# Seven half-size products for the down-projection of the two middle chunks of each FFN, with H and Y kept in memory meanwhile

## The chip, the cores and the metric

The kernel runs on one core of one Trainium2 chip. The metric is the device time of an execution in microseconds (us), as the median of several runs. A NeuronCore has the matrix engine TensorE (PE; its weight loads are listed apart as PEld), the vector engine DVE, the scalar engine ACT, GpSimd (POOL) and the sync engine SP. SBUF is the on-chip memory of 128 partitions, PSUM its accumulator of eight banks, and sixteen DMA engines move data between SBUF and device memory. SP issues the plain transfers here, POOL those that add to what lies at their destination.

## The reference

A decoder trunk of two layers over 528 tokens (16 meta tokens and 512 tokens) with model width 1024 in float32. Each layer has two half-step SwiGLU FFNs of width 2816 around a mixer (gated linear attention in layer 0, sliding-window attention in layer 1). The change touches the FFNs, of which there are four:

```python
def rmsnorm(x, g):
    xf = x.astype(jnp.float32)
    y = xf * lax.rsqrt(jnp.mean(xf * xf, axis=-1, keepdims=True) + EPS)
    return (y * g.astype(jnp.float32)).astype(x.dtype)

def swiglu(x, w_in, w_out):
    gate, up = jnp.split(x @ w_in, 2, axis=-1)
    return (jax.nn.silu(gate) * up) @ w_out
...
    for layer in range(DEPTH):
        g = norm_gains[layer]
        h = h + 0.5 * rmsnorm(swiglu(rmsnorm(h, g[0]), w_ffn_in[layer, 0], w_ffn_out[layer, 0]), g[1])
        hn = rmsnorm(h, g[2])
...
        h = h + rmsnorm(mix, g[3])
        h = h + 0.5 * rmsnorm(swiglu(rmsnorm(h, g[4]), w_ffn_in[layer, 1], w_ffn_out[layer, 1]), g[5])
```

## The kernel before

**Layout.** Everything is kept transposed: 128 rows of the model width on the partitions, tokens along the free axis. `H` (the residual stream) and `Y` (the output of a sub-layer before its norm) are fixed SBUF tiles of eight row blocks x 528 tokens each. All other large operands are tiles of two rows x 528 columns from one pool, `pair_tile` (L162), with `SLOTS` = 32 slots. Matrix products are made in three parts: each operand is split into a rounded high part and the remainder, by an ACT copy and a DVE subtraction, and TensorE runs high x high, low x high and high x low (`mm3s`, L350; one line, L177, issues nearly all matmuls).

**Weights.** All weights are listed in `units` in the order of use. `prefetch` (L316) and `load_unit` (L287) issue their transfers ahead of use into 13 raw tiles of 512 columns; `split_unit` and `split_pair` (L251) split them into pool tiles. `set_ahead` sets how far ahead, and for a pair how many split parts may be alive (`RING` = 10). At most two pairs (`CHAINS`) are in preparation at a time.

**An FFN** (`ffn`, L764) cuts its 22 tiles of the inner width into four chunks (4, 6, 6 and 6 tiles). The first chunk computes gate and up by plain products of two token groups (272 and 256 columns in layer 0, two of 256 or one of 512 in layer 1), while `right_factors` (L832) prepares the fourteen tiles `z` from `H`. The other three chunks use Strassen's scheme in Winograd's form (`class Strassen`, L877): a tile of gate and the tile of up beside it are the two rows of a 2 x 2 block product over the two halves of the model width and the two halves of the tokens, so that seven products of half size (four steps of k, three matmuls each, 264 or 256 columns) take the place of eight. A weight pair is loaded as five raw tiles, two of them summed by accumulating transfers from POOL (L299), and further sums are made on DVE (`add`, L265). `head`, `body` and `tail` issue the seven products of a tile; the head of the next tile is issued between body and tail. The products go onto the banks `a`, `c` (two of each, taken in turns) and `d`; ACT copies them out at L910, L916, L918 and L920, and the job `gated` forms silu(gate) x up and splits it into the tile `hid`.

**Down-projection.** After each chunk `out_steps` (L668) multiplies the chunk's 4 or 6 `hid` tiles with the weights of `w_out` for eight row blocks, over all tokens. The first chunk's result is copied to `Y` (L705), later ones are added to it by DVE (L707). For a chunk of six tiles these are 8 x 6 x 3 = 144 matmuls over each token group. In the last chunk the norm of the output and the residual follow (`Residual.run`, L513), which read `Y` and `H`. In GLA `Y` also holds the values `v`, and in the attention of layer 1 the first four score tiles lie in it.

**Order.** TensorE's order is the program's. The order of program pieces that belong to different tiles comes from `Flow` (L62), a list of jobs with an estimated clock. A job can be delayed by a number it yields, and `flow.wait` runs other jobs until one is done. The other engines run their instructions in the order that the scheduler of the framework made at compile time.

Of the kernel before, what the change touches and what calls it, by code (L numbers as in the profile page):

```python
# [9 lines left out]
F32 = mybir.dt.float32  # L10
# [6 lines left out]
P = 128  # L17
# [14 lines left out]
SLOTS = 32  # L32
# [3 lines left out]
CHAINS = 2  # L36

# [102 lines left out]
def trunk_kernel(ctx: ExitStack, tc, a, out, last_out):  # L140
# [10 lines left out]
    H = cp.tile([P, KD, TOK], F32, name="H")  # L151
    Y = cp.tile([P, KD, TOK], F32, name="Y")
# [16 lines left out]
    def flat(t):  # L169
        return t.rearrange("p a t -> p (a t)")  # L170

# [22 lines left out]
    for layer in range(2):  # L194
        for f in range(2):
            for lo, hi in FF_CHUNKS:
# [3 lines left out]
                if lo < LAST:  # L200
                    units += [a["w_out"][layer, f, m, :, lo * P : hi * P] for m in range(KD)]
                else:
                    units += [a["w_last"][layer, f, i] for i in range(NLAST)]
# [47 lines left out]
    def split_pair(i, raws):  # L251


        r11, r12, r22, s1, s3 = raws
        parts, ready = loaded[i]

        def part(name, src):
            yield from slot(i)
            w = pair_tile(f"w{i}_{name}")
            act.activation(w[:, 0, :512], src, AF.Copy)  # L260
            dve.tensor_tensor(w[:, 1, :512], src, w[:, 0, :512].bitcast(F32), op=ALU.subtract)  # L261
# [10 lines left out]
        add(r11, s1)  # L272
        yield STEP
        yield from part("s2", r11)
        yield STEP
        yield from part("12", r12)
        add(r12, r11)
        yield STEP
        yield from part("s3", s3)
# [7 lines left out]
    def load_unit():  # L287
# [3 lines left out]
        if isinstance(units[i], list):  # L291
            g, u = units[i]
            chains[0] += 1
            a11, a12, a21, a22 = (b[:, c : c + 512] for b in (g, u) for c in (0, 512))
            r11, r12, r22, s1, s3 = raws = [raw_tile(f"raw{i}_{k}") for k in range(5)]
            for r, src in ((s1, a21), (s3, a21), (r11, a11), (r12, a12), (r22, a22)):
                sp.dma_start(r, src)
            for r, src in ((s1, a22), (s3, a11)):
                pool.dma_start(r, src, accum_op=ALU.add)  # L299
            dma_end[0] = max(dma_end[0], flow.clock) + 7 * 512 * 1.5e-3  # L300
            names = ("11", "12", "22", "s1", "s2", "s3", "s4")
            loaded.append(({k: [] for k in names}, {k: Job(None) for k in names}))
            gen = split_pair(i, raws)
# [364 lines left out]
    def out_steps(hid, groups, split_groups, first, finish=None, tailm=0, packed=False, jobs=(), second=(), late=1):  # L668
# [71 lines left out]
        for m in range(KD - tailm):  # L740
# [4 lines left out]
            for gi in range(len(accs)):  # L745
                sq(m, gi)
# [882 lines left out]
```

## Time and profile before

| what | value |
|---|---|
| median of 3 runs | 1875.4 us (1875.31 to 1875.67) |
| the profiled execution's own time | 1875.26 us |
| its span | 1873.5 us |
| instructions | 37758 |
| moved by DMA | 231.37 MB, mean 123 GB/s |
| DMA queues by kind | q1 plain (SP), q0 from POOL, others small |

The page gives busy time, share of the span and number of instructions for each engine, then 40 slices, the DMA queues, the chain of work that ended last (followed back from the end, with the share of the span by engine and by line) and the costliest groups of instructions. A group's row has the line, the engine, the operation, output <- input, the tile form, the count, busy time in us and the mean duration of one in ns, and then the idle time of the engine just before those instructions with what released it. A matmul's duration in ns is its whole way through the array, so the mean is longer than the distance from one matmul to the next. In the chain listed in order of time each row has its start, its length, the engine, the tile written, the line and the number of instructions. In the list of DMA issues the last number is the median time from issue to landing.

### The profile page before, as it was taken

How to read it: one execution, taken by the hardware profiler on the slowest of the kernel's cores; microseconds unless marked ns; L12 is line 12 of the kernel's file. 1: busy time of each engine (PE TensorE's matmuls, PEld its weight loads, DVE VectorE, ACT ScalarE, POOL GpSimd, SP SyncE). 2: the span in 40 equal slices, each digit the busy share in tenths (PEclk: the TensorE clock that was granted, in tenths of full speed). 3: DMA queues.
4: the chain of work that ended last, by engine and by line, in shares of the span. 5: the costliest groups of instructions: out<-in, count | busy, mean ns of one | idle time of the engine just before them, and what ended most of it. 6: DMA issues, size and time to landing. Idle time of an engine off the chain costs nothing.

```text
span 1873.5 us, 37758 instructions
## 1 busy us (share of the span) xinstructions
PE 1864.1 (99%) x14463; PEld 1785.1 (95%) x14463; DVE 1306.0 (70%) x2693; ACT 1022.4 (55%) x2309; POOL 289.2 (15%) x439
## 2 busy tenths in 40 slices
PE   9999999999999999999999999999999999999998
PEld 9999999999999999999999898989988898989898
DVE  7874747767564787474787875757777679758584
ACT  5662636654446566262674563636667866636264
POOL 2101010330001410101033101010220141010102
PEclk9999999999999999999999999999999999999999
DMA  6556565421113255556552456565421224565651
GB/s 209 150 136 150 148 152 151 134 69 57 60 66 113 57 136 140 142 150 150 155 178 57 102 133 172 134 171 146 147 75 52 68 56 120 146 153 157 149 151 46
DMA packets 133381, 231.37 MB, mean 123 GB/s; under 512 B 15312, under 2 KB 27472, under 8 KB 133200
## 3 DMA queue, kind: packets, MB, share of 16 engines
q1 hardware_dynamic: 112032, 190.62, 31.6%
q0 software_dynamic: 20736, 37.76, 12.8%
q8 instruction: 113, 1.85, 0.4%
q14 instruction: 68, 0.56, 0.1%
q10 hardware_dynamic: 432, 0.59, 0.1%
HBM read 226.28 MB, written 2.10 MB: 122 GB/s over the span
## 4 chain that ended last, share of the span: by engine, by line
PE 94%; DVE 3%; ACT 1%; issue 1%; POOL 1%; DMA 0%; SPq 0%; DVEq 0%; POOLq 0%
PE y L177 31%; PE a L177 22%; PE x L177 17%; PE c L177 10%; PE d L177 6%; PE o L177 1%; PE e L177 1%; PE po L177 1%; PE sa L177 1%; PE pt L189 1%; DVE w L242 1%; PE ps L177 0%; ACT w L241 0%; PE sb L177 0%; DVE gu L781 0%
## 5 line engine op out<-in xcount | busy, mean ns | idle before, releaser
L299 POOL DMA_DIRECT2D raw<-in_w_in x144 | 125.8, 908 | 962.7 <-DMA raw<-in_w_in 609.0
L177 PE MATMUL y<-hidl0f,w 128*128 128x256 f32 (+1 forms) x2112 | 262.4, 285 | 1.1 <-DVE hidl0f L454 0.9
L177 PEld LDWEIGHTS y<-hidl0f,w 128*128 128x128 f32 x2112 | 259.3, 188 | 2.2 <-DVE hidl0f L454 1.5
L242 DVE TENSOR_TENSOR w<-raw,w 128x512 fp32r<-128x512 f32 x376 | 234.3, 653 | 35.4 <-ACT w L241 33.0
L261 DVE TENSOR_TENSOR w_s<-raw,w_s 128x512 fp32r<-128x512 f32 x288 | 197.9, 688 | 77.3 <-ACT w_s L260 75.4
L177 PE MATMUL y<-hidl1f,w 128*128 128x512 f32 (+1 forms) x1344 | 250.6, 346 | 0.5 <-DVE hidl1f L454 0.4
L177 PEld LDWEIGHTS y<-hidl1f,w 128*128 128x128 f32 x1344 | 212.2, 188 | 35.0 <-ACT hidl1f L942 0.9
L241 ACT ACTIVATE w<-raw 128x512 fp32r<-128x512 f32 x376 | 206.7, 587 | 52.6 <-PE y L177 34.3
L260 ACT ACTIVATE w_s<-raw 128x512 fp32r<-128x512 f32 x288 | 179.6, 625 | 82.1 <-PE y L177 44.5
L261 DVE TENSOR_TENSOR w<-raw,w 128x512 fp32r<-128x512 f32 x216 | 145.5, 688 | 57.6 <-ACT w L260 53.5
L260 ACT ACTIVATE w<-raw 128x512 fp32r<-128x512 f32 x216 | 130.8, 623 | 44.1 <-PE y L177 42.8
L177 PE MATMUL x<-x_l0m,w 128*128 128x272 f32 (+1 forms) x1152 | 152.1, 288 | 0.0
L707 DVE TENSOR_TENSOR Y<-y,Y 128x256 f32<-128x256 f32 (+2 forms) x175 | 82.0, 475 | 96.4 <-PE y L177 95.4
L177 PEld LDWEIGHTS x<-x_l0m,w 128*128 128x128 f32 x1152 | 143.3, 188 | 2.7 <-issue 1.7
L448 POOL TENSOR_TENSOR acc_post<-acc_post,sq_post 128x256 f32<-128x256 f32 (+1 forms) x77 | 62.8, 816 | 456.0 <-ACT sq_post L447 455.3
L177 PE MATMUL a<-zl0f_t,w_s 128*128 128x264 f32 x864 | 117.4, 285 | 0.0
L177 PE MATMUL a<-zl1f_t,w_s 128*128 128x256 f32 x864 | 113.8, 281 | 0.0
L177 PEld LDWEIGHTS a<-zl0f_t,w_s 128*128 128x128 f32 x864 | 110.3, 188 | 0.0
L177 PEld LDWEIGHTS a<-zl1f_t,w_s 128*128 128x128 f32 x864 | 107.4, 188 | 0.3
L266 DVE TENSOR_TENSOR raw<-raw,raw 128x512 f32<-128x512 f32 x144 | 98.9, 687 | 0.5
L177 PE MATMUL x<-x_l0f,w 128*128 128x256 f32 (+1 forms) x768 | 97.5, 287 | 0.5 <-DVE w L242 0.5
L177 PEld LDWEIGHTS x<-x_l0f,w 128*128 128x128 f32 x768 | 94.8, 188 | 1.3 <-DVE w L242 0.9
(514 smaller groups left out, 3316.9 us busy)
## 6 DMA issues: line engine op xcount, KB each, us to landing
raw<-in_w_in SPq DMA_DIRECT2D x424, 256.0 KB, 3.6
raw<-in_w_in POOLq DMA_DIRECT2D x144, 256.0 KB, 4.9
raw<-in_w_out SPq DMA_DIRECT2D x96, 256.0 KB, 3.3
raw<-in_w_last SPq DMA_DIRECT2D x48, 256.0 KB, 2.9
raw<-in_gla_in SPq DMA_DIRECT2D x48, 256.0 KB, 3.3
raw<-in_w_out SPq DMA_DIRECT2D x64, 128.0 KB, 2.5
raw<-in_gla_out SPq DMA_DIRECT2D x16, 256.0 KB, 2.8
raw<-in_w_q SPq DMA_DIRECT2D x16, 256.0 KB, 4.1
```

The lines of the kernel that those rows point to most:

```text
L177: inst = pe.matmul(o, lhs, rhs, start=start, stop=stop, skip_group_check=onto)
L189: pe.transpose(o, src, ident)
L241: act.activation(w[:, 0, :m], raw[:, :m], AF.Copy)
L242: dve.tensor_tensor(w[:, 1, :m], raw[:, :m], w[:, 0, :m].bitcast(F32), op=ALU.subtract)
L260: act.activation(w[:, 0, :512], src, AF.Copy)
L261: dve.tensor_tensor(w[:, 1, :512], src, w[:, 0, :512].bitcast(F32), op=ALU.subtract)
L266: dve.tensor_tensor(dst, dst, src, op=ALU.add)
L299: pool.dma_start(r, src, accum_op=ALU.add)
L448: pool.tensor_tensor(sums[0][:, :n], sums[0][:, :n], t[:, :n], op=ALU.add)
L707: dve.tensor_tensor(y, p[:, :n], y, op=ALU.add)
```

## The change

- **Seven half-size products for the down-projection.** For the chunks of tiles 4 to 9 and 10 to 15 of each FFN, `hid` is no longer a list of six tiles with their splits. Two neighbouring tiles form a `Step`: the two row halves of a 2 x 2 block, whose columns are the two halves of the tokens. `Step.first` and `Step.second` form the seven right-hand factors from it (four pool tiles f per Step, of six slots with the scratch tiles hk and ht). An item `Down` then computes two row blocks of the output (four items for the eight) by seven products with three steps of k each. Its weight pairs `w_down` are loaded as four raw tiles of 384 columns without accumulating transfers; the sums are made by DVE (`summed` false).
- **Place.** The chunk's four `Down` items come in one list `plan` with the gate-up tiles: after the first tile of the next chunk (`BEFORE_DOWN` = 1). Head, body and tail interleave as before. The first chunk and the last keep the old down-projection.
- **Adding in memory.** `Down` evacuates its banks by ACT into two tiles `t1` and `t2`; POOL issues transfers that add them into `y_sum` and `y_right`, two tensors in device memory (`y_right` is only the right half of the tokens, and the first write of each FFN sets it). `Y` of the first chunk is written to `y_sum` beforehand (`keep`).
- **H and Y.** They are no longer fixed tiles but `Rows`: four pool tiles each, of a pool that now has 40 slots. `H` is written to `h_kept` from `right_factors`, and `H` and `Y` are read back after the tail of the fourth item from the end of the plan (`len(plan) - 4`; three gate-up tiles remain), with `y_right` added to `Y` by POOL. `V` in GLA and the first four score tiles of the attention take pool tiles in place of `Y`.

`class Strassen` keeps its banks and becomes the frame for `Gated` (the former head, body and tail) and `Down`, which share `Item` with `product` and `head`.

```diff
-SLOTS = 32
+SLOTS = 40
...
+BEFORE_DOWN = 1
...
+    dp = ctx.enter_context(tc.tile_pool(name="dp", bufs=1, space=bass.MemoryType.DRAM))
...
+    class Rows:
+        def __init__(self, name):
+            self.name, self.age = name, 0
+            self.fresh()
+
+        def fresh(self):
+            self.age += 1
+            self.tiles = [None] * (KD // 2)
+
+        def pair(self, q):
+            if self.tiles[q] is None:
+                self.tiles[q] = pair_tile(f"{self.name}{self.age}_{q}", F32)
+            return self.tiles[q]
+
+        def __getitem__(self, index):
+            rows, k, cols = (*index, slice(None))[:3]
+            if isinstance(k, slice):
+                assert k.start % 2 == 0 and k.stop == k.start + 2
+                return self.pair(k.start // 2)[rows, :, cols]
+            return self.pair(k // 2)[rows, k % 2, cols]
+
+    H, Y = Rows("H"), Rows("Y")
+    h_kept, y_sum, y_right = (dp.tile([P, KD, TOK], F32, name=f"kept_{nm}") for nm in ("h", "y", "yr"))
...
+                    if ci > 1 and t == lo + BEFORE_DOWN - 1:
+                        units += [[a["w_down"][layer, f, ci - 2, m], a["w_down"][layer, f, ci - 2, m + 1]] for m in range(0, KD, 2)]
+                if lo == 0:
+                    units += [a["w_out"][layer, f, m] for m in range(KD)]
+            units += [a["w_last"][layer, f, i] for i in range(NLAST)]
...
+            r11, r12, s1, r22 = raws
+            s3 = r11
...
+            add(s3, s1)
+            add(s1, r22)
+            s2 = s3
...
+            m = g.shape[-1] // 2
+            summed = m == 512
...
+                raws = [raw_tile(f"raw{i}_{k}")[:, :m] for k in range(4)]
+                for k in (2, 0, 1, 3):
+                    sp.dma_start(raws[k], (a11, a12, a21, a22)[k])
...
+            if keep and m % 2:
+                tok = slice(groups[0][0], groups[-1][0] + groups[-1][1])
+                pool.dma_start(y_sum[:, m - 1 : m + 1, tok], Y[:, m - 1 : m + 1, tok])
...
+        out_proj(hids, groups, x.groups, True, jobs=jobs, keep=True)
+        flow.wait(factors)
+        set_ahead(16, RING)
+        tiles = Strassen(z, halves)
+        plan = []
+        steps = [[Step(tiles, f"{x.name}_{c}{i}") for i in range((hi - lo) // 2)] for c, (lo, hi) in enumerate(FF_CHUNKS[1:3])]
+        for c, (lo, hi) in enumerate(FF_CHUNKS[1:]):
+            for t in range(hi - lo):
+                plan.append(lambda c=c, t=t: Gated(tiles, steps[c][t // 2] if c < 2 else None, t % 2))
+                if c and t == BEFORE_DOWN - 1:
+                    plan += [lambda c=c, q=q: Down(tiles, steps[c - 1], q, c == 1) for q in range(KD // 2)]
+        lo, hi = FF_CHUNKS[-1]
+        hids, jobs = [], []
+
+        def begin(item):
+            t = item()
+            if isinstance(t, Gated) and t.step is None:
+                t.into(new_hid(lo, hids))
+            t.head()
+            return t
+
+        cur = begin(plan[0])
+        for i in range(len(plan)):
+            last = i == len(plan) - 1
+            if last:
+                proj = out_steps(hids, groups, x.groups, False, finish, KD, True, jobs)
+                end = used[0] + NLAST + tail
+            cur.body((lambda: next(proj)) if last else (lambda: None))
+            nxt = None if last else begin(plan[i + 1])
+            job = cur.tail(last)
+            if job is not None:
+                jobs.append(job)
+            cur = nxt
+            if i == len(plan) - 4:
+                H.fresh()
+                Y.fresh()
+                for q in range(KD // 2):
+                    rows, tok = slice(2 * q, 2 * q + 2), slice(o, o + 2 * n2)
+                    sp.dma_start(Y[:, rows, tok], y_sum[:, rows, tok])
+                    sp.dma_start(H[:, rows, tok], h_kept[:, rows, tok])
+                    pool.dma_start(Y[:, rows, right], y_right[:, rows, right], accum_op=ALU.add)
+        set_ahead(32)
...
+        for q in range(KD // 2):
+            rows, tok = slice(2 * q, 2 * q + 2), slice(o, o + 2 * n)
+            sp.dma_start(h_kept[:, rows, tok], H[:, rows, tok])
...
+    class Step:
+        def __init__(self, tiles, name):
+            self.n, self.name, self.parts = tiles.n, name, {}
+            self.done, self.h = Job(None), None
+
+        def rows(self, i):
+            n = self.n
+            if i == 0:
+                self.h, self.t = (pair_tile(f"{nm}{self.name}", F32) for nm in ("hk", "ht"))
+            g, v = (slice(c, c + n) for c in ((n, 0) if i else (0, n)))
+            return self.h[:, i, g], self.h[:, i, v], flat(self.t)[:, (2 + i) * n : (3 + i) * n]
+
+        def split(self, names, src, sign):
+            w = pair_tile(f"f{self.name}_{names[0]}")
+            m = src.shape[-1]
+            act.activation(w[:, 0, :m], src, AF.Copy, scale=sign)
+            if sign == 1.0:
+                dve.tensor_tensor(w[:, 1, :m], src, w[:, 0, :m].bitcast(F32), op=ALU.subtract)
+            else:
+                dve.scalar_tensor_tensor(w[:, 1, :m], src, sign, w[:, 0, :m].bitcast(F32), op0=ALU.mult, op1=ALU.subtract)
+            for i, nm in enumerate(names):
+                self.parts[nm] = [w[:, a, i * self.n : (i + 1) * self.n] for a in range(2)]
+
+        def first(self):
+            self.split(["11"], self.h[:, 0, : self.n], -1.0)
+
+        def second(self):
+            n, h, t = self.n, self.h, flat(self.t)
+            dve.tensor_tensor(
+                t[:, : 2 * n].rearrange("p (a c) -> p a c", c=n),
+                h[:, 0, n : 2 * n].unsqueeze(1).to_broadcast([P, 2, n]), h[:, :, :n], op=ALU.subtract,
+            )
+            yield 0.5
+            self.split(["t1", "t3"], t[:, : 2 * n], 1.0)
+            yield 0.7
+            dve.tensor_tensor(t[:, 2 * n : 3 * n], h[:, 1, :n], t[:, :n], op=ALU.subtract)
+            dve.tensor_tensor(t[:, 3 * n : 4 * n], h[:, 1, n : 2 * n], t[:, 2 * n : 3 * n], op=ALU.subtract)
+            yield 0.7
+            self.split(["t2", "t4"], t[:, 2 * n : 4 * n], 1.0)
+            yield 0.7
+            self.split(["22", "21"], h[:, 1, : 2 * n], -1.0)
+            self.done.finish(flow)
...
+            for k in range(self.nk):
                 wh, wl = (w[:, i, k * P : (k + 1) * P] for i in range(2))
-                xh, xl = (self.z[right][k // 2][:, i, k % 2] for i in range(2))
+                xh, xl = self.right(right, k)
                 mm(bank, wh, xh, first and k == 0, False, not first)
                 mm(bank, wl, xh, False, False, not first)
-                mm(bank, wh, xl, False, k == 3, not first)
+                mm(bank, wh, xl, False, k == self.nk - 1, not first)
...
+                if self.step is not None:
+                    if self.i:
+                        yield from self.step.second()
+                    else:
+                        self.step.first()
+                    return
...
+    class Down(Item):
+        nk = 3
+
+        def __init__(self, tiles, steps, q, new):
+            super().__init__(tiles)
+            self.steps, self.q, self.new = steps, q, new
+            self.t1 = pair_tile(f"dn{self.name}", F32)
+            if q % 2 == 0:
+                tiles.t2 = pair_tile(f"dr{self.name}", F32)
+            self.t2 = tiles.t2[:, q % 2]
+
+        def right(self, name, k):
+            flow.wait(self.steps[k].done)
+            return self.steps[k].parts[name]
+
+        def body(self, between):
+            n = self.n
+            self.product(self.c, "s1", "t1", True)
+            act.activation(self.t2[:, n : 2 * n], self.c, AF.Copy, scale=-1.0)
+            self.product(self.a, "s2", "t2", False)
+            act.activation(self.t2[:, :n], self.a, AF.Copy)
+            self.product(self.d, "12", "21", False)
+            act.activation(self.t1[:, 0, :n], self.d, AF.Copy)
+            self.product(self.a, "s3", "t3", False)
+            act.activation(self.t1[:, 1, n : 2 * n], self.a, AF.Copy, scale=-1.0)
+
+        def tail(self, last):
+            n, o = self.n, self.tiles.o
+            rows, tok, right = slice(2 * self.q, 2 * self.q + 2), slice(o, o + 2 * n), slice(o + n, o + 2 * n)
+            self.product(self.c, "s4", "22", False)
+            act.activation(self.t1[:, 0, n : 2 * n], self.c, AF.Copy)
+            self.product(self.a, "22", "t4", False)
+            act.activation(self.t1[:, 1, :n], self.a, AF.Copy, scale=-1.0)
+            released[0] += 1
+            t2 = self.t2[:, : 2 * n].rearrange("p (a c) -> p a c", c=n)
+            if self.new:
+                pool.dma_start(y_right[:, rows, right], t2)
+            else:
+                pool.dma_start(y_right[:, rows, right], t2, accum_op=ALU.add)
+            pool.dma_start(y_sum[:, rows, tok], self.t1[:, :, : 2 * n], accum_op=ALU.add)
...
+            V = Rows("V")
...
+                    scores[i] = flat(pair_tile(f"s{u}_{hf}", F32))[:, :580]
...
+    c["w_out"] = wo[:, :, :, :, : FF_CHUNKS[0][1]].reshape(2, 2, KD, P, FF_CHUNKS[0][1] * P)
+    c["w_down"] = np.stack([
+        np.concatenate([wo[:, :, :, :, lo + i : hi : 2] for i in range(2)], axis=4) for lo, hi in FF_CHUNKS[1:3]
+    ], axis=2).reshape(2, 2, 2, KD, P, 6 * P)
```

More of the change, by code (lines that the diff above doesn't have):

```diff
@@ L195, in trunk_kernel @@
         for f in range(2):
-            for lo, hi in FF_CHUNKS:
+            for ci, (lo, hi) in enumerate(FF_CHUNKS):
                 for t in range(lo, hi):
@@ L832, in right_factors @@
+        set_ahead(32)
+        cap[0] = min(end, len(units))
+        for _ in proj:
+            pass
     def right_factors(x, halves, z, plain):
@@ L889, in product, with __init__ @@
+    class Item:
+        def __init__(self, tiles):
+            self.tiles, self.n, self.d = tiles, tiles.n, tiles.d
+            i = tiles.count % 2
+            tiles.count += 1
+            self.a, self.c = tiles.a[i], tiles.c[i]
+            self.pair, self.name = next_pair(), used[0]
+        def product(self, bank, left, right, first):
+            parts, ready = self.pair
             flow.wait(ready[left])
             w = parts[left][0]
-            for k in range(4):
+            for k in range(self.nk):
```

201 lines of the change are left out of this document (98 added, 103 removed).

## The prediction

> **What bounds the kernel now.** I read the page's first part, then the chain that ended last, then the stretches.
>
> ```profile
> PE 1864.1 (99%) x14463; PEld 1785.1 (95%) x14463; DVE 1306.0 (70%) x2693; ACT 1022.4 (55%) x2309; POOL 289.2 (15%) x439
> PE 94%; DVE 3%; ACT 1%; issue 1%; POOL 1%; DMA 0%; SPq 0%; DVEq 0%; POOLq 0%
> ```
>
> TensorE is busy for 1864.1 of 1873.5 us and is 94% of the chain: what it does not have to multiply is saved, as long as operands still arrive. The 9.4 us in which it is idle are all that better overlap could win. The chain in order of time (start, length, what) gives its pace, for the first layer's third chunk and for the same chunk of the second layer:
>
> ```profile
> 185.37 2.92 PE a L177 x24
> 226.27 2.91 PE a L177 x24
> 242.80 33.21 PE y L177 x273
> 282.01 2.92 PE a L177 x24
> ...
> 1175.56 2.83 PE a L177 x24
> 1215.24 2.83 PE a L177 x24
> 1236.42 26.85 PE y L177 x114
> 1269.09 2.83 PE a L177 x24
> ```
>
> From 185.37 to 226.27 lie four tiles of a gate-up product by sevenths: 10.225 us each, and with 7 x 12 = 84 matmuls a tile, 121.7 ns per matmul of 264 columns. In the second layer it is 39.68 / 4 = 9.92 us, 118.1 ns for 256 columns. A chunk is 282.01 - 185.37 = 96.64 us, of which six tiles take 61.35; its down-projection takes 35.29 (288 matmuls). In the second layer 93.53 - 59.52 = 34.01 us (144 matmuls of 512 columns).
>
> **The half-size products.** One chunk of a down-projection is now four row pairs x 7 products x 9 matmuls = 252 of 264 (256) columns. At the chain's pace that is 30.67 us, or 29.76 in the second layer: 4.62 and 4.25 us less. Each layer has four such chunks: 4 x (4.62 + 4.25) = **35.5 us**. The groups by form would say otherwise:
>
> ```profile
> L177 PE MATMUL y<-hidl1f,w 128*128 128x512 f32 x768 | 180.5, 394 | 0.5 <-DVE hidl1f L454 0.4
> L177 PE MATMUL a<-zl1f_t,w_s 128*128 128x256 f32 x864 | 113.8, 281 | 0.0
> ```
>
> 180.5 / 768 = 0.235 us for 512 columns, 113.8 / 864 = 0.132 for 256, so that two halves would be dearer than a whole and the second layer would win only 144 x 0.235 - 252 x 0.132 = 0.6 us a chunk, 4 x (4.62 + 0.6) = 20.9 us in all. But such a busy time counts the tail of each product together with the start of the next bank's; the spacing in the chain has no such overlap, and I take it. Nine matmuls in place of twelve change nothing: each has its own weight load either way.
>
> The span lies 1.76 us under that execution's 1875.26, which itself is 0.14 under the median of 1875.4. With everything hidden: 1875.26 - 35.5 = 1839.8.
>
> **What DVE and ACT get to do.** Windows by stage (length, then busy time of PE, PEld, DVE, ACT, POOL, clock, DMA share):
>
> ```profile
> 185.40:236.50 51.10, 51.10 (x422) 51.10 (x421) 40.56 (x73) 32.42 (x71) 3.46 (x4) 1.00 0.52 145
> 236.50:282.00 45.50, 45.50 (x376) 45.50 (x375) 21.81 (x45) 12.18 (x25) 7.01 (x8) 1.00 0.64 152
> ```
>
> ```profile
> 207.71 0.43 DVE L923 TENSOR_TENSOR c<-a,c 128x264 f32<-128x264 f32 x1
> 208.05 0.68 DVE L261 TENSOR_TENSOR w<-raw,w 128x512 fp32r<-128x512 f32 x1
> 208.65 0.69 DVE L261 TENSOR_TENSOR w_s<-raw,w_s 128x512 fp32r<-128x512 f32 x1
> ```
>
> Back to back, a DVE operation on 264 columns holds the engine 0.34 us and one on 512 columns 0.60; I put 0.47 for 384 and 0.62 for 528. A Down item has 7 weight splits and 4 additions of 384 columns: 5.2 us of its 63 x 121.7 ns = 7.67 us. A Step (two gate-up tiles) has 0.34 + 4 x 0.62 + 2 x 0.34 = 3.5 us in place of two splits of 0.62: +2.3. Removed in a chunk are 8 split pairs of 512 and 256 (7.5 us) and 16 additions into Y (5.4). DVE goes from 62.4 of 96.6 us to 62.4 - 12.9 + 4 x 5.2 + 3 x 2.3 = 77.2 of 92.0 us, 84%. ACT:
>
> ```profile
> L241 ACT ACTIVATE w<-raw 128x512 fp32r<-128x512 f32 x312 | 182.6, 622 | 18.9 <-PE y L177 14.9 <-PE e L177 2.0 <-DVE hidl1f L943 1.5
> L241 ACT ACTIVATE w<-raw 128x256 fp32r<-128x256 f32 x64 | 26.4, 412 | 33.7 <-PE y L177 19.4 <-PE a L177 11.8 <-ACT c L933 1.1
> L918 ACT ACTIVATE c<-a 128x264 f32<-128x264 f32 x36 | 13.7, 380 | 0.1
> ```
>
> A split of 384 is some 0.50 us (between 0.41 and 0.585), an evacuation 0.38: 6.2 us for a Down item. With about 1 us more a Step, ACT has 44.6 - 8.0 + 24.8 + 3 = 64 of 92 us. Neither becomes the bound on average, and TensorE's matmuls cover both. Locally three places are tight:
> - The first Down item comes one gate-up tile after the last Step's second tile. Its second product needs t1 after 4 + 2 products of twelve and one of nine, 9.9 us; the Step's own work after that tile is 3.8 us of DVE, and the rest of DVE's work there 79% of 9.9. Together that is 1.7 us too much, unless weight splits made ahead (ten slots) give way. Between 0 and 1.7 us, I take 0.5; eight starts: 4 us.
> - `a` is emptied by ACT while TensorE does the one product "12", and then "s3" goes onto it. The evacuation ends 0.42 us before that today:
>
> ```profile
> 204.81 0.37 ACT L918 ACTIVATE c<-a 128x264 f32<-128x264 f32 x1
> 205.60 1.63 PE L177 MATMUL a<-zl0f_t,w_s 128*128 128x264 f32 x12
> ```
>
>  With nine matmuls "s3" comes 0.37 us sooner and ACT's split before it is 0.1 shorter: 0.15 us is left. Between 0 and 0.2 us lost per item; 0.1 x 32 = 3 us.
> - Tiles: 14 of z, 12 f, ten weight parts, hk, ht and f11 of the next Step, two t1 and one or two t2 make 42 or 43 for 40 slots. The ring then runs two or three short; a product frees one every 1.10 us. It is in the 0.5 above.
>
> **What the DMA engines get to do.**
>
> ```profile
> q1 hardware_dynamic: 112032, 190.62, 31.6%
> q0 software_dynamic: 20736, 37.76, 12.8%
> ```
>
> Share x 1873.5 / MB: a plain MB takes 3.11 us of all 16 engines, an accumulating one 6.35. A gate-up pair (1.311 plain, 0.524 accumulated) is 7.40 us. Old chunk: 6 x 7.40 + 8 x 0.393 x 3.11 = 54.2 of 96.6 us; the windows' 0.52 and 0.64 give 55.7, so this holds. New: 44.4 + 4 x 0.786 x 3.11 + 4 x (0.541 + 0.270) x 6.35 = 74.8 of 92.0 us. Accumulating in memory is nowhere in this trace. Its nearest rows are a write to memory and an accumulation in SBUF:
>
> ```profile
> out<-H SPq DMA_DIRECT2D x4, 256.0 KB, 2.8
> raw<-in_w_in POOLq DMA_DIRECT2D x144, 256.0 KB, 4.9
> ```
>
> Below: the price of a plain transfer, 64.3 us. Above: a read, a write and an accumulation one after the other, about twice 6.35, 95.4 us, which is more than the chunk. I take 6.35 (nearest: same queue, same operation) and no cost. On POOL's queue each of these transfers waits for ACT's last evacuation, and raw additions for the next pairs stand behind it; those are issued well ahead, as the next rows show.
>
> **H and Y back.** SP's issues before the last chunk's end:
>
> ```profile
> 282.08 24.32 SPq L297 DMA_DIRECT2D raw<-in_w_in  x12
> 306.67 20.79 SPq L310 DMA_DIRECT2D raw<-in_w_last  x12
> ```
>
> The last pair's weights leave SP by 306.4; TensorE begins that tile at about 324 (the chunk starts at 276.0, the sixth head comes 7.3 + 4 x 10.225 later). Ahead of them now stand 8 transfers of 0.541 MB (13.4 us) and 4 accumulations of 0.270 MB (6.9 us). 17.9 - 13.4 leaves 4.5 us, about one landing; and SP can start the eight while it waits for raw buffers. Between 0 and 20.3 us per FFN; nearest 0, I take 0.8, 3 us in all. H and Y going out (4.3 MB per FFN, 13.4 us) lie in the first chunk, with DMA at half load; nothing waits for them but slots.
>
> Sum: 1839.8 + 4 + 3 + 3 = **1850 us**; own range 1840 to 1860.
>
> **Rivals.**
> 1. All is hidden: 1840. For it: TensorE shows no idle time in either window. Against it: the three tight places.
> 2. Small waits at every bank: four evacuations in each of 32 Down items, 0.2 us each, 26 us: 1866. For it the 0.15 us left; against it that ACT is below 70%.
> 3. Slower: the accumulations into y_sum and y_right saturate the DMA engines in the two chunks that follow. It decides from 1.83 times the price above (92.0 us in a chunk), eats the gain at 2.05 times, and at 2.25 times a chunk is 100.6 us, 8.6 more, eight times: 1909. For it: 81% already at the known price. Against it: weights are issued some 18 us ahead.
> 4. The reload stands in front of the last weights. From 8.9 us per FFN the gain is gone; all of 20.3 exposed gives 1839.8 + 81 = 1921.
> 5. A wait for one landing at each of the eight starts and four reloads, and matmuls at a slower pace after it:
>
> ```profile
> raw<-in_w_in SPq DMA_DIRECT2D x424, 256.0 KB, 3.6
> ...
> L1444 PE MATMUL busy<-ones 128*128 128x128 f32 x26 | 5.8, 423 | 1.0 <-DVE eps L1496 1.0
> L189 PE MATMUL pt<-ident,s 128*128 128x128 f32 x48 | 7.2, 272 | 0.0
> ```
>
>  The opening's matmuls take 0.22 us, the same shape later 0.15: 26 of them cost 1.9 us more. Twelve pauses of 3.6 + 1.9 us are 66: 1906. Against it, the granted clock is 1.00 in every stretch I read. The Trainium skill (TensorE: Matmul & The Clock Gate, section on HAM oscillation) says that a kernel whose matmuls wait over some 3.4 us for data falls back to half rate each time; no run here shows such a pause in mid-kernel, only the slow opening agrees.
> 6. It does not do what it says: slots freed by H and Y are eaten by Steps, and weights come as late as the saving is large: no change, 1875.
>
> **How the numbers follow.** Forecast 0.50, all hidden 0.13, small waits 0.12, saturation 0.12, reload 0.06, slow pace 0.05, no change 0.02. This measurement tells 0.2% (3.8 us) from nothing. Faster: 0.50 + 0.13, 0.08 of the small waits and 0.01 of the saturation, 0.72. Same: the 0.02, and 0.03 of the small waits, 0.05. Slower 0.23. The range from 1837 (1840 less part of today's idle time) to 1885 holds the first three cases and the mild end of the saturation and reload.
>
> **What would show it.** Right: 252 matmuls per middle chunk in about 30.7 us, PE idle time near 20 us in all, DVE about 77%. Wrong on DMA: raw issues on POOL landing later than 8 us, PE idle before the gate-up tiles after a Down. Wrong on the reload: idle time before the last pair of an FFN. Wrong on banks: PE waiting for the copies of `a` in a Down item. A chunk longer than 96.6 us would overturn the forecast.

## The result, and the profile after

The changed kernel takes 1919.06 us (median of four runs, 1915.92 to 1919.62) against 1875.54 us beside it: a ratio of 1.0229, 95% interval [1.0211, 1.0246]. It is slower by 43.5 us where 25 were to be gained. The profiled execution took 1915.92 us. Busy time and the chain that ended last, from the changed kernel's page:

```profile
PE 1854.5 (97%) x14743; PEld 1794.1 (94%) x14743; DVE 1428.6 (75%) x2933; ACT 1148.5 (60%) x2677; POOL 383.4 (20%) x535
PE 69%; DVE 11%; DMA 11%; ACT 5%; issue 3%; POOL 1%; SPq 0%; DVEq 0%; ACTq 0%; POOLq 0%
```

TensorE's share of the chain fell from 94% to 69%, and DMA now has 11%. Against "everything hidden" (1839.8 us, PE busy 1864.1 - 35.5 = 1828.6, idle 9.4) the execution lost 76.1 us in two ways: PE idle for 1914.1 - 1854.5 = 59.6 us, 50.2 more, and busy 25.9 us longer than its matmuls need. What TensorE waited for (line, tile, releaser: us in all, times, longest):

```profile
PE a L201 <- ACT dr L1115: 23.1, 10, 3.7
PE a L201 <- DVE c L1062: 15.2, 5, 4.4
PE a L201 <- ACT dn L1119: 4.7, 1, 4.7
PE a L201 <- ACT w_s L282: 2.9, 2, 2.5
```

The rows released by ACT are the Down items, some 31 us. Seven of the eight chunks have such a wait of over 2 us, the first of them 23 to 27 us after the chunk's first Down product. The DVE row is the last gate-up tile but one of each FFN (in the first FFN also the last), behind the reload of H and Y. One Down wait, in the changed kernel's timeline (start, length, engine, line, what; in brackets the engine's idle time before it and what ended it):

```profile
881.73 1.24 POOL L1134 DMA_DIRECT2D kept_y<-dn  x1
...
885.37 1.25 PE L201 MATMUL a<-fl0f_t,w_s 128*128 128x264 f32 x9
...
885.85 0.52 ACT L282 ACTIVATE w_s<-raw 128x384 fp32r<-128x384 f32 x1
...
886.45 1.26 PE L201 MATMUL d<-fl0f,w 128*128 128x264 f32 x9
...
889.61 0.94 ACT L282 ACTIVATE w<-raw 128x384 fp32r<-128x384 f32 x2 [3.24 <-DMA kept_y<-dn]
...
890.46 0.37 ACT L1115 ACTIVATE dr<-a 128x264 f32<-128x264 f32 x1
...
890.88 1.36 PE L201 MATMUL a<-fl0f_t,w_s 128*128 128x264 f32 x9 [3.17 <-ACT dr L1115]
```

At 889.61 ACT splits a weight. Neither its input nor its result has to do with `dn`, yet it waited 3.24 us for a transfer out of `dn`, issued at 881.73. What they can share is the pool slot: a slot last held by `dn` is free only when the addition into memory has landed, 7.9 us after its issue. ACT runs its instructions in the scheduler's order, so the copy that empties bank `a` (890.46) stood behind the split, though its product had ended at about 886.6; and TensorE stood behind the copy.

What follows such a wait, in windows of the changed kernel (length, then busy time of PE, PEld, DVE, ACT, POOL with counts, clock, DMA share):

```profile
891.00:892.00 1.00, 1.00 (x9) 1.00 (x10) 0.96 (x3) 0.00 (x0) 0.00 (x0) 1.00 1.16 272
892.00:893.00 1.00, 1.00 (x7) 1.00 (x7) 0.41 (x2) 0.71 (x3) 0.95 (x2) 0.60 1.18 228
893.00:894.00 1.00, 1.00 (x7) 1.00 (x6) 0.59 (x2) 0.78 (x3) 1.00 (x1) 0.50 1.09 215
```

The granted clock falls to 0.50. The clock record has ten such spells before the last 2 us of the kernel, 3.413 us each, seven behind Down waits and three behind reload waits. At half rate they lose 10 x 3.413 / 2 = 17.1 us, two thirds of PE's 25.9. The other 8.8 us are also there in the last run below, which has no spell.

The reload in the second FFN, from the chain in order of time (start, length, what):

```profile
922.33 9.42 DMA H<-kept_h
...
931.81 15.03 DMA raw<-in_w_last
946.84 0.02 issue
946.86 0.63 ACT w L266
...
948.93 0.44 DVE c L1062
949.36 0.04 issue
949.41 2.37 PE a L201 x12
```

`w_last` are the weights of the last down-projection. In this chain SP's first issue of them follows the landing of a load of H, and their own landing takes 15 us; ACT's split (L266) waits for them, DVE's subtraction for ACT, and behind that on DVE stands the addition (L1062) that empties a bank for TensorE. TensorE itself uses these weights only from 956.90 on. The twelve matmuls then take 2.37 us in place of 12 x 121.7 ns = 1.46. From the list of DMA issues (count, KB each, median us to landing):

```profile
raw<-in_w_in POOLq DMA_DIRECT2D x144, 256.0 KB, 5.5
...
raw<-in_w_last SPq DMA_DIRECT2D x48, 256.0 KB, 8.5
...
kept_y<-dn POOLq DMA_DIRECT2D x16, 528.0 KB, 8.5
...
Y<-kept_y SPq DMA_DIRECT2D x8, 528.0 KB, 12.2
...
H<-kept_h SPq DMA_DIRECT2D x8, 528.0 KB, 13.0
```

The queues by kind, from its page:

```profile
q1 hardware_dynamic: 122016, 216.18, 34.4%
q0 software_dynamic: 39680, 76.10, 21.8%
```

### The profile page after: what moved, and what is told of

Its sections match the earlier page's. It is cut to its first block, busy times and chain, and to the rows that moved or that the text cites. A ratio compares the mean times of both kernels' runs of the same rounds, so it can differ in the third digit from the quotient of the medians.

```text
span 1914.1 us, 39248 instructions
## 1 busy us (share of the span) xinstructions
PE 1854.5 (97%) x14743; PEld 1794.1 (94%) x14743; DVE 1428.6 (75%) x2933; ACT 1148.5 (60%) x2677; POOL 383.4 (20%) x535
## 3 DMA queue, kind: packets, MB, share of 16 engines
q0 software_dynamic: 39680, 76.10, 21.8%
## 4 chain that ended last, share of the span: by engine, by line
PE 69%; DVE 11%; DMA 11%; ACT 5%; issue 3%; POOL 1%; SPq 0%; DVEq 0%; ACTq 0%; POOLq 0%
PE a L201 18%; PE x L201 16%; PE y L201 16%; PE c L201 9%; PE d L201 5%; DMA raw<-in_w_last 3%; DMA kept_y<-dn 3%; DMA raw<-in_w_in 2%; DVE raw L288 2%; DVE w L283 2%; DVE w_s L283 2%; ACT w_s L282 1%; DMA kept_yr<-dr 1%; PE o L201 1%; DMA H<-kept_h 1%
## 5 line engine op out<-in xcount | busy, mean ns | idle before, releaser
L283 DVE TENSOR_TENSOR w_s<-raw,w_s 128x512 fp32r<-128x512 f32 (+1 forms) x416 | 268.1, 648 | 138.9 <-ACT w_s L282 134.7
L282 ACT ACTIVATE w_s<-raw 128x512 fp32r<-128x512 f32 (+1 forms) x416 | 245.4, 592 | 123.9 <-DVE raw L288 106.3
L283 DVE TENSOR_TENSOR w<-raw,w 128x512 fp32r<-128x512 f32 (+1 forms) x312 | 200.0, 646 | 26.9 <-ACT w L282 24.0
L267 DVE TENSOR_TENSOR w<-raw,w 128x512 fp32r<-128x512 f32 x248 | 165.7, 702 | 51.7 <-ACT w L266 50.5
L282 ACT ACTIVATE w<-raw 128x512 fp32r<-128x512 f32 (+1 forms) x312 | 181.3, 586 | 11.5 <-DMA kept_y<-dn 7.3
L288 DVE TENSOR_TENSOR raw<-raw,raw 128x512 f32<-128x512 f32 (+1 forms) x272 | 170.2, 626 | 4.1
L266 ACT ACTIVATE w<-raw 128x512 fp32r<-128x512 f32 x248 | 142.1, 620 | 25.3 <-DMA raw<-in_w_last 23.7
L201 PE MATMUL y<-hidl0f,w 128*128 128x272 f32 (+1 forms) x960 | 120.0, 285 | 1.2 <-DVE hidl0f L502 1.0
L201 PEld LDWEIGHTS y<-hidl0f,w 128*128 128x128 f32 x960 | 117.9, 188 | 2.2 <-DVE hidl0f L502 1.6
L201 PE MATMUL y<-hidl1f,w 128*128 128x256 f32 (+1 forms) x768 | 115.2, 310 | 0.4 <-DVE hidl1f L502 0.4
```

The source lines that it names most:

```text
L201: inst = pe.matmul(o, lhs, rhs, start=start, stop=stop, skip_group_check=onto)
L266: act.activation(w[:, 0, :m], raw[:, :m], AF.Copy)
L267: dve.tensor_tensor(w[:, 1, :m], raw[:, :m], w[:, 0, :m].bitcast(F32), op=ALU.subtract)
L282: act.activation(w[:, 0, :m], src, AF.Copy)
L283: dve.tensor_tensor(w[:, 1, :m], src, w[:, 0, :m].bitcast(F32), op=ALU.subtract)
L288: dve.tensor_tensor(dst, dst, src, op=ALU.add)
```

## The experiments

All are edits of the changed kernel. Times are medians of two to ten executions, with the ratio to the kernel before and its 95% interval.

**H read later.** H's four loads of each FFN move behind the weights of the last down-projection.

```diff
-                H.fresh()
...
-                    sp.dma_start(H[:, rows, tok], h_kept[:, rows, tok])
...
         set_ahead(32)
...
+        H.fresh()
+        for q in range(KD // 2):
+            rows, tok = slice(2 * q, 2 * q + 2), slice(o, o + 2 * n2)
+            sp.dma_start(H[:, rows, tok], h_kept[:, rows, tok])
```

> H is read back only after the last tile of the FFN, behind the weights w_last in SP's order; everything else as in the changed kernel. If the reload's eight transfers stand in front of w_last and ACT and DVE wait for w_last (the changed kernel's last tile of each FFN: TensorE idle 1.57, 4.05, 3.92 and 4.40 us, with a half-clock spell behind three of them), that idle time goes and with it about 14 + 3 x 1.7 = 19 us: some 1899 us. If the wait there comes from the accumulations of y_right into Y or from a full DMA in general, it stays within 3 us of 1919.

1900.72 us, 1.0136 [1.0107, 1.0165]: 18.3 us less. The waits of PE for `DVE c` are gone from its list, those in the Down items stay:

```profile
PE a L201 <- ACT dr L1117: 23.8, 9, 4.5
PE a L201 <- ACT dn L1121: 5.8, 1, 5.8
```

`w_last` takes as long to land as before (8.7 us from issue by the median, 8.5 before), but it is issued sooner: in the second FFN 3.2 us after the first load of Y (923.90 to 927.09), in the changed kernel 10.0 us after it (921.85 to 931.81).

**No y_right back into Y.** The four additions of POOL into `Y` per FFN are left out, H is read early.

```diff
-                    pool.dma_start(Y[:, rows, right], y_right[:, rows, right], accum_op=ALU.add)
```

> The changed kernel (1919 us) without the 16 transfers that add y_right to Y at the reload; the output lacks that half's part. Reading H late removed the wait at w_last, and so did leaving y_right out altogether with H read early. If the four additions of 0.27 MB per FFN, on top of the eight loads, are what makes w_last late, TensorE's waits before the last products (1.57 to 4.40 us) fall under 1 us each and the time to some 1900 us. If they need the shorter waits in Down items instead, the waits stay and the time is 1910 us or more.

1902.29 us, 1.0142 [1.0112, 1.0171]; the wait for `DVE c` shrinks from 15.2 to 2.7 us, and the last weights land 5.9 us after issue, not 8.5. So twelve transfers per FFN around these weights are too many: taking away four loads lets the weights start sooner, taking away four additions lets them land sooner, and either one cures the wait.

**A ring of 8.** `RING` 10 becomes 8, two parts fewer in the 40 slots.

> The ring of live weight parts is eight in place of ten, so that tiles asked for in the Down items fall from 42 or 43 to 40 or 41 of 40 slots. Theory of full slots (a weight split on ACT waits for the slot of a dn tile whose transfer into memory has not landed, with the copies that empty TensorE's bank behind it): the idle time of 31 us in Down items falls to some 10 us, the total to about 1885 us. Rival, late weights by full DMA queues: a shorter ring makes it worse, 1925 us or more.

1909.29 us, 1.0182 [1.0128, 1.0236]. If two slots too few were all, the Down waits had to shrink; they stayed (ACT's rows in PE's list 21.0 and 4.7 us). The reload waits fell from 15.2 to 6.8 us. What the 10 us of the median are made of isn't shown: the two executions lie at 1905.02 and 1913.57, and the profiled one is the slower, 2.4 us under the profiled one of the changed kernel.

**No tile held for the transfer.** The transfers into memory carry an f tile that is alive anyway, so the sums lack the products.

```diff
-            pool.dma_start(y_sum[:, rows, tok], self.t1[:, :, : 2 * n], accum_op=ALU.add)
+            pool.dma_start(y_sum[:, rows, tok], f[:, :, : 2 * n], accum_op=ALU.add)
```

> The transfers into y_sum and y_right carry a tile of right-hand factors that is alive anyway, so that dn and dr hold their slots only until ACT has written them; number, size and place of the transfers stay. The output lacks the chunk's products. Theory of full slots: idle time in Down items under 8 us in place of 31 and at most one half-clock spell there, about 1880 us. Rival (DMA engines busy with accumulations, raw weights late): idle time stays over 20 us, 1910 us.

1897.54 us, 1.0119 [1.0090, 1.0148]. No wait over 0.3 us is left in the Down items. But this doesn't tell the slots from the traffic, because the edit also moved the transfers: they no longer wait for `dn`, and a chunk's eight are issued in one burst, 38 us or more ahead of its Down items (109.1 to 113.8 us in the first chunk, whose first Down product comes at 152.2). Those into `y_sum` then take 14.8 and 16.6 us, and new waits stand in gate-up items, where ACT's splits wait for accumulating weight loads (19.7 us in four waits); the DVE row is the reload's:

```profile
PE a L201 <- DVE c L1064: 12.7, 4, 3.9
PE a L201 <- ACT htl1f L1059: 12.5, 2, 7.1
PE a L201 <- ACT htl0f L1059: 4.7, 2, 2.4
```

**As the last, without the additions into y_sum.**

> As the run without hold, and the 32 accumulations of 0.5 MB into y_sum are left out as well (the output lacks them). It gives the price of that DMA traffic by itself. Theory of full slots: within 5 us of the run without hold. Rival (traffic): some 25 us faster than that run.

1875.29 us, 0.9996 [0.9984, 1.0007], 22.3 us less, which was the sign named for the traffic: eight transfers at once do cost time. The waits of the middle chunks are gone but for 0.4 us and less, while the reload's `DVE c` still has 13.9 us: it is not an effect of late Down items.

**POOL's order.** H late; the accumulating loads of the next weights are issued only when the program comes to split their pair, so that no transfer of `dn` should stand behind them.

> On top of reading H back late (1900.7 us): POOL's additions to raw weights are issued when the pair's loads should have landed, no longer ahead of them, so that the transfer of a finished dn tile does not stand behind a raw addition that waits for its load. If that standing behind is what keeps the slots (in the changed kernel a dn tile finished at 172.5 was sent at 179.1 and landed at 187.1), idle time in Down items falls from 30 us to under 18 and the total to about 1885 us. If the transfer itself takes the time, within 4 us of 1900.7.

1899.04 us, 1.0123 [1.0093, 1.0152], and the Down waits as with H late alone (26.3 and 5.5 us). But the edit hardly changed POOL's order:

```profile
172.16 0.39 ACT L1130 ACTIVATE dn<-a 128x264 f32<-128x264 f32 x1 [0.33 <-PE a L201]
...
178.17 0.90 POOL L291 DMA_DIRECT2D raw<-in_w_in  x1 [10.08 <-DMA raw<-in_w_in]
178.78 1.20 POOL L1137 DMA_DIRECT2D kept_y<-dn  x1
```

The `dn` filled at 172.55 still stands behind an addition to a raw tile and leaves 6.2 us later (6.3 with H late alone). What that order costs is therefore not shown; it can only lengthen the time for which a slot is held.

**No y_right.** H late; `dr` and `y_right` go, DVE adds the right half inside `dn` when it empties the bank (two more DVE additions an item).

```diff
-            act.activation(self.t1[:, 0, n : 2 * n], self.c, AF.Copy)
+            right = self.t1[:, 0, n : 2 * n]
+            dve.tensor_tensor(right, self.c, right, op=ALU.add)
```

> On top of reading H back late (1900.7 us): the right half's two terms are added by DVE when the banks are emptied, in place in dn; y_right, the dr tiles, 32 transfers out and 16 back go, and one or two tiles fewer ask for slots. Theory of full slots: 41 tiles for 40 slots, idle time in Down items from 30 us to about 12 and four spells less, some 1878 us. Theory of DMA traffic: 12.7 of 38.3 MB of POOL's additional transfers go, a third of the idle time and of the slow spells with it: about 1886 us. DVE gets 0.7 us more per Down item of 7.7 us, which it has.

1883.48 us, 1.0047 [1.0036, 1.0059]. With a third of the Down traffic gone, splits still wait for transfers of `dn`, in ACT's list:

```profile
ACT w_s L282 <- DMA kept_y<-dn: 24.0, 8, 5.8
...
ACT w L282 <- DMA kept_y<-dn: 8.4, 6, 2.2
```

**Own slots for dn.** As the last, but `dn` has three slots of its own, the pool 37, the ring 8.

```diff
-            self.t1 = pair_tile(f"dn{self.name}", F32)
+            self.t1 = hp.tile([P, 2, TOK], F32, tag="dn", name=f"dn{self.name}", bufs=3)
```

> As the run without y_right, with dn in three slots of its own, 37 for the rest and a ring of eight: no weight split can then wait for a transfer into memory, only the next but two dn tile can. Theory of full slots: idle time in Down items under 8 us, no or one half-clock spell there, about 1862 us. Theory of DMA traffic: as the run without y_right, within 4 us.

1855.73 us, 0.9892 [0.9863, 0.9921] (again, with more runs, 1854.77, 0.9890 [0.9875, 0.9905]). TensorE's waits for ACT's copies (`dn`) fall to 1.9 us, though the transfers land later than in the changed kernel (9.5 and 9.7 us).

**Its control: the ring of 8 with 40 common slots.**

> The run without y_right (1883.5 us) with a ring of eight and nothing else: dn stays in the common 40 slots. It parts the two things that the run with own slots changed together. If what counts is the number of tiles that ask for slots (now 39 for 40), waits in Down items are gone: about 1858 us. If what counts is that a weight split's slot may be one that a dn tile had before, whatever the number, it stays between 1875 and 1887 us.

1884.28 us, 1.0053 [1.0037, 1.0069]: the ring did nothing, the own slots 29 us. By the count in the expectation 39 tiles asked for 40 slots here, and the waits stayed: too few slots are not the cause either.

**Two own slots in place of three.**

> The run with own slots (1855.7 us) with two slots for dn in place of three, 38 for the rest. A dn tile is being filled for some 6.5 us, waits for POOL 1 to 2 us and is in transfer for 9.5: 17 us or more, while items come every 7.8 us. Two slots should then hold up the third and fourth Down item of each chunk by some 2 us each: 16 x 2 us and a few half-clock spells, about 1890 us, with TensorE waiting for ACT's copies into dn. If the transfers were harmless, 1856 us.

1895.9 us, 1.0108 [1.0088, 1.0128]. The wait moves to the copies themselves, in ACT's list:

```profile
ACT dn L1111 <- DMA kept_y<-dn: 26.7, 13, 3.4
```

A tile is written for one item (7.7 us) and then held 8.4 to 9.0 us by its transfer, over 16 us in all, so two slots cannot quite carry an item every 7.7 us and three can.

**A ring of 9 with three own slots.**

> The run with own slots with a ring of nine in place of eight: 14 + 12 + 9 + 3 = 38 tiles for 37 slots. All of them are now freed by engines and not by transfers, so one too many costs at most one product's time here and there: 1853 to 1860 us.

1852.96 us, 0.9880 [0.9864, 0.9897]: the best version, 22.7 us under the kernel before (1875.64 beside it). Its page and three rows of its timeline:

```profile
PE 1835.6 (99%) x14743; PEld 1778.5 (96%) x14743; DVE 1450.7 (78%) x2997; ACT 1129.5 (61%) x2613; POOL 331.0 (18%) x487
```

```profile
174.13 1.25 PE L201 MATMUL d<-fl0f,w 128*128 128x264 f32 x9
...
176.47 1.25 PE L201 MATMUL a<-fl0f,w 128*128 128x264 f32 x9
...
181.94 1.25 PE L201 MATMUL d<-fl0f,w 128*128 128x264 f32 x9
```

From 176.47 to 181.94 lie five products: 5.47 / 45 = 121.6 ns a matmul. A whole item of seven, from one `d` to the next (174.13 to 181.94), takes 7.81 us or 124.0 ns a matmul, and its two products d and s3 (174.13 to 176.47) 130 ns. The clock record has no spell before the kernel's last microsecond.

**The same, with H read early.**

> The fastest version so far (own slots, ring of nine, no y_right: 1853.0 us) with H read back where the changed kernel reads it, ahead of w_last. If the two causes are independent, this brings back four waits of 1.5 to 4.5 us in the last tile of an FFN and the half-clock spells behind them: 1853 + 10 to 19, some 1868 us. If the wait at w_last came only from Down items that ran late, 1853 to 1857 us.

1853.31 us, 0.9881 [0.9865, 0.9898]. The early reload costs nothing here, against what was expected. The last weights land after 5.7 us.

**Own slots for dn alone, y_right kept.** Three slots for `dn`, 37 for the rest with `dr` among them, ring 8, H early.

> The changed kernel with dn in three slots of its own, 37 for the rest with dr among them, a ring of eight, y_right and the early reload kept: as much of the memory traffic as in the changed kernel. Theory of slots: most of the 31 us of idle time in Down items goes, dr still holds some of the common slots, and the reload's waits stay (14 us and some spells): about 1885 us. Theory of traffic: over 1905 us.

1908.28 us, 1.0174 [1.0144, 1.0203], which spoke for the traffic. But ACT's list shows that `dr` had taken the place of `dn`:

```profile
ACT dr L1113 <- DMA kept_yr<-dr: 11.2, 2, 5.7
...
ACT w L282 <- DMA kept_yr<-dr: 4.9, 1, 4.9
...
ACT w_s L282 <- DMA kept_yr<-dr: 4.6, 2, 3.1
```

So four runs settle slots against traffic, with H late.

**Five own slots for both dn and dr**, 35 for the rest, ring 6; all transfers and arithmetic of the changed kernel:

> The changed kernel with H read back late, where the tiles of both sums, dn and dr, share five slots of their own; 35 slots are left for the others and the ring of weight parts is cut to 6. All transfers and all arithmetic are the changed kernel's, y_right included. Theory of shared slots: no weight split waits for a transfer of dn or dr, the 30 us of idle time in Down items and their slow spells go, and 1900.7 falls to about 1860 (up to 1875 if six weight parts are too few). Rival, the traffic of y_right and the copies of its tiles cost the time themselves: waits in the Down items stay and the time stays over 1885.

1869.15 us, 0.9967 [0.9955, 0.9980]. **Its control without y_right**, three own slots, 35 for the rest, ring 6:

> Control for the run before: the version without y_right, dn in three own slots, with 35 other slots and a ring of 6 in place of 37 and 8 or 9. It tells what fewer slots and a shorter ring cost by themselves. If nothing: 1853 to 1856, as with 37 slots. If weights then come late: 1860 to 1875, and the run before is to be read against that.

1874.05 us, 0.9993 [0.9984, 1.0003]. The smaller pool and ring cost 19 us; with y_right the kernel is not slower but 5 us faster. **The short ring with common slots**:

> Control for the run with five own slots: the changed kernel with H read back late, a ring of 6 weight parts, and all tiles in 40 common slots. If sharing is the cause, weight splits still stand behind transfers of dn or dr, the idle time in the Down items stays over 15 us and the time stays over 1890. If it was the short ring that removed the waits, the idle time goes and the time is 1865 to 1875 here too.

1901.0 us, 1.0135 [1.0118, 1.0152]. **Four own slots for both, 36 for the rest, ring 8**:

```diff
-SLOTS = 40
+SLOTS = 36
...
-RING = 10
+RING = 8
...
-            self.t1 = pair_tile(f"dn{self.name}", F32)
+            self.t1 = hp.tile([P, 2, TOK], F32, tag="down", name=f"dn{self.name}", bufs=4)
...
-                tiles.t2 = pair_tile(f"dr{self.name}", F32)
+                tiles.t2 = hp.tile([P, 2, TOK], F32, tag="down", name=f"dr{self.name}", bufs=4)
```

> As the run with five own slots for dn and dr, but four of them, 36 for the rest and a ring of 8. If four are enough, about 1860, because the longer ring gives back some of the 19 us that the short one costs. If not (with two own slots for dn alone the copies out of the banks waited 27 us), ACT's copies into dn and dr wait for landings: 1880 to 1900.

1859.97 us, 0.9917 [0.9903, 0.9932]. From "H read later" it differs in the slots and in the ring (8 for 10), and it is 40.7 us faster; that a shorter ring with common slots gains nothing is the run before. Its page, the waits of its TensorE, and its transfers:

```profile
PE 1837.4 (99%) x14743; PEld 1779.3 (96%) x14743; DVE 1428.4 (77%) x2933; ACT 1148.7 (62%) x2677; POOL 382.5 (21%) x535
```

```profile
PE a L201 <- ACT dr L1117: 4.3, 8, 1.0
...
PE a L201 <- ACT dn L1121: 1.6, 1, 1.6
```

```profile
kept_y<-dn POOLq DMA_DIRECT2D x16, 528.0 KB, 10.3
```

The transfers land 1.8 us later than in the changed kernel, and nothing in the Down items waits over 1.6 us. It was where the tiles lay.

## Why the prediction was wrong

- **35.5 us fewer matmuls: right in the pace, too large in sum.** Product behind product takes 121.6 ns a matmul against the 121.7 reckoned with, but a whole item 124.0. PE busy fell by 28.5 us in the best version (1864.1 to 1835.6), and no spell of half clock lies in it: 7.0 us are missing, in part around s3. The reading by the groups, 20.9 us, is refuted.
- **Eight starts, 4 us: the step that failed.** "The ring then runs two or three short; a product frees one every 1.10 us. It is in the 0.5 above." I priced the 42 or 43 tiles for 40 slots as a number, as if each slot came free when a product ends. A slot of `dn` or `dr` comes free at a landing, 7.1 to 8.8 us after an issue by the medians of the changed kernel, and the next to want it may be a weight split, with the emptying of TensorE's banks behind it on ACT. This was worth 40.7 us; the number of parts in the ring was not it (with H late 1901.0 at 6 against 1900.72 at 10). I had asked who waits on POOL's queue behind these transfers, not who waits for the memory they hold.
- **The reload, 3 us: mis-sized, and by another path.** My bounds held it (0 to 20.3 us per FFN); 18.3 / 4 = 4.6 us is the measured cost of H's early place. I had the weights of the last gate-up pair late; late were those of the down-projection behind it, which TensorE didn't need yet, and the orders of ACT and DVE passed the wait on. "SP can start the eight while it waits for raw buffers" was too hopeful: with the reload the DMA share, 0.64 in such a stretch before, is over 1 there (window of the changed kernel). The share alone doesn't make the wait: with H late it is 1.05 in the same window, and TensorE is never idle in it.

```profile
915.00:950.00 35.00, 30.95 (x255) 30.73 (x254) 23.59 (x43) 19.26 (x41) 8.20 (x8) 1.00 1.05 310
```

- **Saturation, 0 us for it: right about the price.** q0 grew by 38.34 MB and 21.8% x 1914.1 - 12.8% x 1873.5 = 177.5 us: 4.6 us per MB, plain writes among them, not over 6.35. Raw additions land 5.5 us after issue, under the 8 that I had set. But a DMA share with room left says nothing of a transfer's own length: the 8.5 us from issue to landing are what held the slots.
- **Banks, 3 us: about right.** Where slots are apart, the list has 4.3 us for the copies of `a`, and the slower pace around s3, 130 ns a matmul in the best version, comes on top. In the changed kernel the same row has 23.1 us, and read as I proposed ("wrong on banks") it would have blamed ACT's pace.
- **DVE**, 77% foreseen: 75%, and 77% where TensorE does not wait.
- **Rival 5 came nearest**, at 0.05: waits for a landing, and a slower pace after. It had twelve, at the starts and the reloads; there were fourteen of over 1 us, nine of them inside the Down items. That its 66 us are near the 50.2 of idle time and 17.1 of half clock is luck in part. The rule of the Trainium skill (TensorE: Matmul & The Clock Gate, section on HAM oscillation), that a matmul engine idle over some 3.4 us falls to half rate, agrees with the ten spells here, but for its threshold: waits of 2.50 and 3.11 us were enough (below). I had held against it a clock of 1.00 in stretches without waits, which says nothing of what a wait does.
- **Together**: own slots 40.7 us, H late 18.3, and 1859.97 are left, 10 over the forecast, of which 8.8 are PE busy time (1837.4 against 1828.6). Why the reload is free without y_right and with own slots even when early is shown only as far as that its weights then land in 5.7 us.

## What to carry to other kernels

A tile that a transfer empties is held until the landing; give such tiles slots of their own, as many as fit the time of writing plus landing into the interval between them, and never a slot whose next user stands in front of an urgent instruction on its engine. When the profile names a transfer as what released an instruction that doesn't touch its data, look for a shared buffer before looking for bandwidth. Count a wait in the middle of a matmul stream with what may follow it: here most waits of 3 us were followed by 3.413 us at half clock, 1.7 us more.

## What the chip showed that I had not expected

In these runs spells at half clock in mid-kernel last 3.413 us or twice that, and behind which wait they come is not decided by its length alone. Two waits of the changed kernel:

```profile
179.06 2.35 PE L201 MATMUL a<-fl0f_t,w_s 128*128 128x264 f32 x9 [3.73 <-ACT dr L1115]
...
1286.54 1.33 PE L201 MATMUL a<-fl1f_t,w_s 128*128 128x256 f32 x9 [3.22 <-ACT dr L1115]
```

After 3.73 us nine matmuls took 2.35 us, after 3.22 the clock held; but one of 3.11, one of 3.17 and one of 2.50 were followed by a spell. The shortest that was is in the control with the ring of 8 and common slots, where the spell begins 0.2 us after this start:

```profile
1680.89 2.13 PE L201 MATMUL a<-fl1f_t,w_s 128*128 128x256 f32 x9 [1.72 <-ACT dn L1113]
```

With H late the seven spells each lasted 6.83 us and lose 23.9 us in place of 17.1. PE busy time rose by only 1.9 us there, while idle time fell by 15.9; the difference isn't accounted for.

An addition of 0.5 MB into memory takes 7.7 to 10.3 us from issue to landing, by the medians, in the versions that send `dn`, with or without y_right's traffic (7.7 to 9.8 without), while the mean of POOL's added transfers, 4.6 us of all engines per MB, is below the 6.35 of additions into SBUF.
